# Hybrid decoder layer on one core: a separate transfer path for the modulation of k-tiles 4 to 15

## The chip, the cores and the metric

One core of a Trainium2 chip runs the whole layer as one program. The metric is device time in microseconds, from the start of the program to its end; the median of the runs counts. TensorE multiplies matrices (PE in the profile, with its weight loads as PEld), VectorE (DVE) and ScalarE (ACT) do the elementwise work, GpSimd (POOL) and SyncE (SP) issue transfers here, and POOL builds a few masks as well.

## The reference, cut to what matters

The layer is one block of a decoder: 256 tokens of width 2048, all in float32. A conditioning vector c gives six vectors of modulation, and the first two of them, shift and scale, act on the normalised input of every projection:

```python
mod = (jax.nn.silu(c) @ w_ada[l] + b_ada[l]).reshape(B, N_MOD, 1, D)
sh1, sc1, gt1, sh2, sc2, gt2 = (mod[:, j] for j in range(N_MOD))

h = rmsnorm(x, g_mix[l]) * (1.0 + sc1) + sh1
z = h @ w_in[l]
```

z is cut into the inputs of three token mixers (mLSTM, differential attention, stick-breaking attention) and their gates. Their outputs are projected, gated, summed and projected again, a gated residual is added, and a modulated MLP with a causal convolution follows. w_ada is 2048 x 12288, so the columns that sh1 and sc1 need are 33.5 MB in float32; no column of h can be made before its shift and scale are known, and each needs all 2048 rows of w_ada.

## The kernel before

The width of 2048 is cut into 16 k-tiles of 128. h is kept transposed, one 128 x 256 tile per k-tile, as a high and a low part in a rounded float format; weights are split in the same way, and each product is made of three matmuls (high by high, high by low, low by high). `weights` (L318) loads up to four k-tiles of 512 columns, one megabyte, into one of three buffers (`rawp`), ScalarE writes the high part (L330) and VectorE the low part (L332). A buffer is free again when both have read it.

The modulation takes no TensorE time for its products: `ada_mac` (L208) multiplies the rows of one k-tile of w_ada by the matching entries of silu(c), one number per partition, and adds them up on VectorE over all 16 row tiles; `ada_sums` (L226) then sums over the partitions with one-column matmuls, writes shift and scale, and `make_h` (L438) makes h for the k-tiles concerned.

The columns come in this order. `ada_first(0)` and `ada_first(2)` (L239) give k-tiles 0 and 1, and 2 and 3. `ada_quad` (L260) gives four k-tiles at a time, for k0 = 4, 8 and 12: eight buffers of one megabyte, each of two row tiles of 128 x 1024, filled by two transfers on SyncE's queue (L267), and sixteen multiply-adds. These buffers come from the same `rawp` as the weights, so weights and modulation rotate through the same three in the order of the program, and both go out on SyncE's queue. The accumulators are the two halves of `quads` (slot 4).

Since h arrives piece by piece, the first 13 column blocks of w_in (`first`, L488) are visited several times. `visit` (L531) calls `partial` for a range of blocks up to the k-tile that is there: up to 2, then 4, 8, 12 and 16; the last visit is the loop at L863. The first two blocks keep their sums in PSUM (`kept`), the others add theirs into SBUF (L522). `partial` drives the modulation on if h isn't written far enough (L503).

Two queues of generators, `ada` and `side`, are advanced by `tick` (L200), which is called after each group of four k-tiles and after each block. `rates` say how many steps per tick, 0.72 to 2.1 for `ada` during the visits. Program order is a priority: the planner that comes with the tile framework simulates the program, places each instruction on its engine when the engine is free and its inputs are there in its own time, and fixes an order for each engine. `tc.issue_after` adds a rule to it: an instruction comes after another one on the same engine. The order is kept on the chip: an engine whose next instruction has to wait, waits.

`late_vectors` (L138) loads the small vectors (gains, convolution weights, gate biases, the four lambda vectors) with small transfers on POOL's queue into slot 3 (`rows2`), turns them into columns with five transposes on TensorE, a copy on ScalarE (L164), and computes lambda. It is put on `side` after the third visit (L540). Slot 3 held the first half of x before, and holds the output of stick-breaking attention (`osh`, L550) after it.

Of the kernel before, what the change touches and what calls it, by code (L numbers as in the profile page):

```python
# [10 lines left out]
F32 = mybir.dt.float32  # L11
# [6 lines left out]
P = 128  # L18
S = 256
NT = S // P  # L20
D = 2048
KD = D // P
# [17 lines left out]
def kernel(  # L40
# [6 lines left out]
    nc = tc.nc  # L47
    x2d, out2d = x[0], out[0]
    w_ada, w_in, w_out, w_up, w_down = w_ada[0], w_in[0], w_out[0], w_up[0], w_down[0]
# [4 lines left out]
    rawp = ctx.enter_context(tc.tile_pool(name="rawp", bufs=3))  # L54
# [8 lines left out]
    def slot(i, name):  # L63
        n = NT * MH * (MDH + 1) + 8 if i == 2 else 2048
        return slots.tile([P, n], F32, tag=f"s{i}", name=name)
# [7 lines left out]
    def sidewide(name):  # L73
        return tmp.tile([P, 512], F32, tag="sidewide", name=name, bufs=4)
# [4 lines left out]
    V, A, T = nc.vector, nc.scalar, nc.tensor  # L79
# [58 lines left out]
    def late_vectors():  # L138
        rows = slot(3, "rows2")
        rowsB, rowsC = rows[0:27, 0:P], rows[0:64, P:2 * P]  # L140
        rowsD = rows[0:NF, 2 * P:5 * P].rearrange("k (j p) -> k j p", j=3)
        def ld(*args):
            with tc.issue_after(state["load"].ins):
                nc.gpsimd.dma_start(*args)

        ld(rowsB[0:16], g_ffn[0].rearrange("(k p) -> k p", p=P))
        ld(rowsB[16:24], g_mout[0].rearrange("h (k p) -> (h k) p", p=P))
        ld(rowsB[24:25], g_dsub)
        for r in range(2):
            ld(rowsB[25:26, r * 64:(r + 1) * 64], g_dq)  # L150
            ld(rowsB[26:27, r * 64:(r + 1) * 64], g_dk)
        ld(rowsC, w_mconv[0].rearrange("j (k p) -> (j k) p", p=P))
        ld(rowsD, w_ffconv[0].rearrange("j (k p) -> k j p", p=P))
        ld(bif, b_gate_if.rearrange("o (g h) -> h (o g)", h=MH))
        lamv = rows[0:1, 640:896].rearrange("o (v d) -> o v d", v=4)
        for i, lv in enumerate((lam_q1, lam_k1, lam_q2, lam_k2)):
            ld(lamv[:, i, :], lv)
        yield
        pv = adaps.tile([P, 512], F32, tag="adaps", name="pv")
        T.transpose(pv[:, 0:27], rowsB, ident[:27, :27])  # L160
        T.transpose(pv[:, 27:91], rowsC, ident[:64, :64])
        for j in range(3):
            T.transpose(pv[:, 91 + NF * j:91 + NF * (j + 1)], rowsD[:, j, :], ident[:NF, :NF])
        A.copy(cols, pv[:, 0:223])  # L164
        yield
        V.tensor_scalar(gsub_c, gsub_c, 1.0 - LAM_INIT, None, ALU.mult)
        V.tensor_scalar(gdq_c, gdq_c, 64.0 ** -0.5, None, ALU.mult)

        lp = rows[0:1, 896:1024].rearrange("o (v d) -> o v d", v=2)
        V.tensor_tensor(lp, lamv[:, 0::2, :], lamv[:, 1::2, :], ALU.mult)  # L170
        ls = const.tile([1, 2], F32, name="ls")
        V.tensor_reduce(ls, lp, AX.X, ALU.add)
        A.activation(ls, ls, AF.Exp)
        nl = const.tile([1, 1], F32, name="nl")
        V.scalar_tensor_tensor(nl, ls[:, 1:2], -LAM_INIT, ls[:, 0:1], ALU.add, ALU.subtract)
        yield
        plam = adaps.tile([P, 512], F32, tag="adaps", name="plam")
        T.matmul(plam[:, 0:1], lhsT=ones[0:1, :], rhs=nl, start=True, stop=True)
        V.tensor_copy(nlam, plam[:, 0:1])


    side = deque()
    ada = deque()
    state = {"ada": 0.0, "side": 0.0, "split": None, "load": None, "hold": None, "h": 0, "started": False}
# [13 lines left out]
    rates = {"ada": 0.0, "side": 1.0}  # L198
# [9 lines left out]
    def ada_mac(accs, raw, kt0, nk):  # L208
        for k in range(nk):
            kt = kt0 + k  # L210
            acc = accs[kt % len(accs)]
            if kt < len(accs):
                V.tensor_scalar(acc, raw[:, k, :], ccol[:, kt:kt + 1], None, ALU.mult)
            else:
                state["mac"] = V.scalar_tensor_tensor(acc, raw[:, k, :], ccol[:, kt:kt + 1], acc, ALU.mult, ALU.add)  # L215
# [10 lines left out]
    def ada_sums(accs, k0, nk):  # L226

        pm = adaps.tile([P, 512], F32, tag="adaps", name="pm")
        for i, acc in enumerate(accs):
            for k in range(2 * nk):  # L230
                T.matmul(pm[:, k:k + 1], lhsT=acc[:, k * P:(k + 1) * P], rhs=ones[:, 0:1],  # L231
                         start=k + i == 0, stop=i == len(accs) - 1, skip_group_check=True)
        ks = slice(k0, k0 + nk)
        V.tensor_tensor(b1[:, ks], pm[:, 0:nk], bsh1_c[:, ks], ALU.add)
        V.tensor_tensor(a1[:, ks], pm[:, nk:2 * nk], bsc1_c[:, ks], ALU.add)
        V.tensor_tensor(a1[:, ks], a1[:, ks], gmix_c[:, ks], ALU.mult)
        make_h(k0, k0 + nk)

    def ada_first(k0):  # L239

        accs = [adap.tile([P, 512], F32, tag="acc", name="acc", bufs=2)]
        if k0 == 0:
            accs.append(sidewide("acc2"))
        for q in range(4):
            raw = rawp.tile([P, 4, 512], F32, tag="raw", name="raw")
            step = 2 if k0 == 0 and q == 3 else 4
            for j in range(0, 4, step):
                for i in range(2):
                    r0, c0 = q * 512 + j * P, i * D + k0 * P
                    with tc.issue_after(state["load"].ins) if k0 else nullcontext():  # L250
                        load = nc.sync.dma_start(raw[:, j:j + step, i * 256:(i + 1) * 256],  # L251
                                                 w_ada[r0:r0 + step * P, c0:c0 + 256].rearrange("(k p) f -> p k f", p=P))
            if k0 == 0:
                state["load"] = load
            with tc.issue_after(state["first"].ins) if k0 == 2 and q == 0 else nullcontext():
                ada_mac(accs, raw, 4 * q, 4)
            yield
        ada_sums(accs, k0, 2)

    def ada_quad(k0, acc):  # L260

        for q in range(8):
            raw = rawp.tile([P, 2, 1024], F32, tag="raw", name="raw4")
            for i in range(2):
                r0, c0 = q * 256, i * D + k0 * P
                with tc.issue_after(state["load"].ins):
                    nc.sync.dma_start(raw[:, :, i * 512:(i + 1) * 512],  # L267
                                      w_ada[r0:r0 + 256, c0:c0 + 512].rearrange("(k p) f -> p k f", p=P))
            for k in range(2):
                ada_mac([acc], raw[:, k:k + 1, :], 2 * q + k, 1)  # L270
                yield
        ada_sums([acc], k0, 4)

    def ada_late(comp, g):
# [11 lines left out]
    def ada_columns(comp, bcol, dst, gcol=None):  # L286
        for g in range(4):
            for acc in ada_late(comp, g):
                yield
            pm = partition_sums(acc)  # L290
            ks = slice(4 * g, 4 * g + 4)
            V.tensor_tensor(dst[:, ks], pm[:, 0:4], bcol[:, ks], ALU.add)
            if gcol is not None:
                V.tensor_tensor(dst[:, ks], dst[:, ks], gcol[:, ks], ALU.mult)
# [229 lines left out]

    kept = {}
    quads = slot(4, "quads")
    ada.append(ada_first(2))
    ada.extend(ada_quad(k0, quads[:, (i % 2) * 1024:(i % 2 + 1) * 1024]) for i, k0 in enumerate((4, 8, 12)))
    done = [0] * 13

    def visit(cis, kt1, rate):  # L531
        rates["ada"] = rate
        for ci in cis:
            partial(ci, done[ci], kt1)
            done[ci] = kt1
# [1 line left out]
    visit(range(0, 9), 2, 0.72)  # L537
    visit(range(9, 13), 4, 2.1)
    visit(range(0, 9), 4, 1.1)
    side.append(late_vectors())  # L540
    rates["side"] = 0.4
    visit(range(0, 10), 8, 1.72)
    visit(range(10, 13), 12, 1.36)
    visit(range(0, 7), 12, 1.36)
# [312 lines left out]
    def ada_rest():  # L857
        yield from ada_columns(3, bsh2_c, b2)
        yield from ada_columns(4, bsc2_c, a2, gffn_c)

    ada.append(ada_rest())
    rates["side"] = 2.4
    for ci in range(13):  # L863
        partial(ci, done[ci], 16)
# [20 lines left out]
    for ch in range(2):  # L885
        acc = gemm("T", hact, w_in, 0, C_MO + ch * 512, 512, 0, KD)
# [6 lines left out]
    for ch in range(2):  # L893
        acc = gemm("T", hact, w_in, 0, C_MV + ch * 512, 512, 0, KD)
# [5 lines left out]
    for t, col0, f0 in ((mqT, C_MQ, 0), (mkT, C_MK, 8)):  # L900
        for ch in range(2):
            acc = gemm("H", h1act, w_in, 0, col0 + ch * 512, 512, 0, KD)
# [44 lines left out]
    for ch in range(4):  # L947
        acc = gemm("T", mact, w_out, 0, ch * 512, 512, 0, KD)
# [17 lines left out]
        for k2 in range(2):  # L966
            pb = bank("px2")
            for tt in range(NT):
                for j in range(2):
                    k = 4 * ch + 2 * k2 + j  # L970
                    T.transpose(pb[:, j * S + tt * P:j * S + (tt + 1) * P], x2[tt][:, k * P:(k + 1) * P], ident)
            for j in range(2):
                k = 4 * ch + 2 * k2 + j
# [10 lines left out]
    k = 0  # L984
# [17 lines left out]
    for half, (c0, c1) in enumerate(((0, 6), (6, NCH))):  # L1002
        ath = [slots.tile([P, 8, S], F32R, tag=f"s{i}", name=f"ath{i}") for i in (0, 3, 4)]
        atl = [slots.tile([P, 8, S], F32R, tag=f"s{i}", name=f"atl{i}") for i in (5, 6, 7)]
        for ch in range(c0, c1):
# [21 lines left out]
            i, j0 = (ch - c0) // 2, ((ch - c0) % 2) * 4  # L1027
# [12 lines left out]
        for n in range(4):  # L1040
            acc = gemm("T", act, w_down, c0 * 512, n * 512, 512, 0, 4 * (c1 - c0))
# [37 lines left out]
```

## Time and profile before

| | us |
|---|---|
| runs, median of 3 | 1796.61 (1796.43 to 1796.66) |
| the profiled execution | 1796.63 |
| its span, from first to last instruction | 1794.9 |
| TensorE busy | 1757.0 (98%) |
| VectorE busy | 1325.2 (74%) |
| ScalarE busy | 909.9 (51%) |
| POOL busy | 16.3 (1%) |
| DMA traffic | 423.31 MB, mean 236 GB/s |

Times inside the execution are counted from the start of the span. A busy matmul includes time in which it waits in the pipeline, so a row of busy time is not a row of peak work. "Idle before" is put down to whatever released the engine last. Transfers are shown on the queue of the engine that issues them, with the time from issue to landing.

### The profile page before, as it was taken

How to read it: one execution, taken by the hardware profiler on the slowest of the kernel's cores; microseconds unless marked ns; L12 is line 12 of the kernel's file. 1: busy time of each engine (PE TensorE's matmuls, PEld its weight loads, DVE VectorE, ACT ScalarE, POOL GpSimd, SP SyncE). 2: the span in 40 equal slices, each digit the busy share in tenths (PEclk: the TensorE clock that was granted, in tenths of full speed). 3: DMA queues.
4: the chain of work that ended last, by engine and by line, in shares of the span. 5: the costliest groups of instructions: out<-in, count | busy, mean ns of one | idle time of the engine just before them, and what ended most of it. 6: DMA issues, size and time to landing. Idle time of an engine off the chain costs nothing.

```text
span 1794.9 us, 23561 instructions
## 1 busy us (share of the span) xinstructions
PE 1757.0 (98%) x9101; PEld 1510.3 (84%) x9101; DVE 1325.2 (74%) x1784; ACT 909.9 (51%) x1238; POOL 16.3 (1%) x44
## 2 busy tenths in 40 slices
PE   6999999999999999999999999999999999999998
PEld 5888999888778887888888878888888888888887
DVE  6889766888988678777896577888875556666654
ACT  6533344666565566544444555555553345555432
POOL 2000000000000000000000000000000000000000
PEclk8999999999999999999999999999999999999999
DMA  9989855776777657778896547778755555555563
GB/s 337 356 279 314 299 181 177 241 259 234 247 247 258 199 201 267 237 261 288 308 327 211 186 160 254 248 256 279 269 200 188 199 194 190 190 189 188 187 212 116
DMA packets 219728, 423.31 MB, mean 236 GB/s; under 512 B 9026, under 2 KB 31674, under 8 KB 219104
## 3 DMA queue, kind: packets, MB, share of 16 engines
q1 hardware_dynamic: 217328, 417.44, 68.7%
q0 software_dynamic: 1008, 2.23, 0.4%
q10 hardware_dynamic: 1280, 2.14, 0.3%
q8 instruction: 71, 1.16, 0.3%
q14 instruction: 41, 0.34, 0.0%
HBM read 419.68 MB, written 2.10 MB: 235 GB/s over the span
## 4 chain that ended last, share of the span: by engine, by line
PE 91%; DVE 3%; DMA 3%; ACT 1%; issue 1%; SPq 0%; DVEq 0%; ACTq 0%
PE gp L379 51%; PE acch L365 31%; PE kept L381 2%; PE gp L381 2%; DMA raw<-in_w_in_dram 2%; DVE lo L332 1%; DMA raw<-in_w_ada_dram 1%; DVE quads L215 1%; ACT hi L330 1%; PE psc L650 0%; SPq L251 0%; PE pm L231 0%; DVE acc L215 0%; PE pr L309 0%; PE pmg L848 0%
## 5 line engine op out<-in xcount | busy, mean ns | idle before, releaser
L332 DVE TENSOR_TENSOR lo<-raw,hi 128x1024 fp32r<-128x1024 f32 (+1 forms) x608 | 724.1, 1207 | 344.8 <-ACT hi L330 308.4
L330 ACT CAST hi<-raw 128x1024 fp32r<-128x1024 f32 (+1 forms) x608 | 617.2, 1039 | 608.5 <-PE gp L379 367.0
L379 PE MATMUL gp<-hi,h 128*128 128x512 f32 (+1 forms) x1600 | 408.1, 385 | 6.1 <-ACT hi L330 5.4
L365 PE MATMUL acch<-h,hi 128*128 128x512 f32 x1664 | 404.2, 392 | 1.8 <-DVE h L994 1.8
L365 PEld LDWEIGHTS acch<-h,hi 128*128 128x128 f32 x1664 | 304.7, 189 | 59.9 <-DVE h L994 2.0
L379 PEld LDWEIGHTS gp<-hi,h 128*128 128x128 f32 x1600 | 296.6, 188 | 59.3 <-ACT hi L330 7.2
L379 PE MATMUL gp<-lo,h 128*128 128x512 f32 (+1 forms) x800 | 227.1, 384 | 0.0
L365 PEld LDWEIGHTS acch<-h,lo 128*128 128x128 f32 x1664 | 217.5, 191 | 11.1
L365 PE MATMUL acch<-h,lo 128*128 128x256 f32 x1664 | 220.7, 282 | 0.0
L215 DVE SCALAR_TENSOR_TENSOR acc<-araw,ccol,acc 128x512 f32<-128x512 f32 x240 | 179.1, 747 | 6.5 <-DMA araw<-in_w_ada_dram 4.8
L379 PEld LDWEIGHTS gp<-lo,h 128*128 128x128 f32 x800 | 149.5, 188 | 25.6 <-issue 0.7
L379 PE MATMUL gp<-hi,atl 128*128 128x512 f32 x352 | 136.9, 389 | 0.0
L379 PE MATMUL gp<-hi,ath 128*128 128x512 f32 x352 | 136.8, 389 | 0.0
L379 PE MATMUL gp<-lo,ath 128*128 128x512 f32 x352 | 105.7, 389 | 0.0
L379 PEld LDWEIGHTS gp<-hi,ath 128*128 128x128 f32 x352 | 66.1, 188 | 13.8
L379 PEld LDWEIGHTS gp<-lo,ath 128*128 128x128 f32 x352 | 66.1, 188 | 13.7
L379 PEld LDWEIGHTS gp<-hi,atl 128*128 128x128 f32 x352 | 66.0, 188 | 13.7
L215 DVE SCALAR_TENSOR_TENSOR quads<-raw,ccol,quads 128x1024 f32<-128x1024 f32 x45 | 57.6, 1280 | 2.1 <-DMA raw<-in_w_ada_dram 1.6
L379 PE MATMUL gp<-hi,mgl 128*128 128x512 f32 x128 | 50.3, 393 | 0.0
L379 PE MATMUL gp<-hi,mgh 128*128 128x512 f32 x128 | 50.0, 392 | 0.0
L381 PE MATMUL kept<-h,hi 128*128 128x256 f32 x256 | 42.0, 305 | 5.1 <-ACT hi L330 2.0
L1019 DVE SCALAR_TENSOR_TENSOR y<-gsum,cols,y 128x255 f32<-128x255 f32 (+1 forms) x88 | 41.7, 479 | 4.4 <-ACT y L1017 4.0
(355 smaller groups left out, 1560.8 us busy)
## 6 DMA issues: line engine op xcount, KB each, us to landing
raw<-in_w_in_dram SPq DMA_DIRECT2D x98, 1024.0 KB, 5.1
raw<-in_w_up_dram SPq DMA_DIRECT2D x88, 1024.0 KB, 5.1
araw<-in_w_ada_dram SPq DMA_DIRECT2D x128, 512.0 KB, 5.9
raw<-in_w_down_dram SPq DMA_DIRECT2D x44, 1024.0 KB, 5.1
raw<-in_w_ada_dram SPq DMA_DIRECT2D x62, 512.0 KB, 5.6
raw<-in_w_branch_dram SPq DMA_DIRECT2D x24, 1024.0 KB, 5.2
raw<-in_w_in_dram SPq DMA_DIRECT2D x25, 880.0 KB, 4.7
raw<-in_w_out_dram SPq DMA_DIRECT2D x16, 1024.0 KB, 5.1
```

Of the source, the lines that this page charges most:

```text
L215: state["mac"] = V.scalar_tensor_tensor(acc, raw[:, k, :], ccol[:, kt:kt + 1], acc, ALU.mult, ALU.add)
L330: A.copy(hi[:, :, :n], raw[:, k0:k0 + 2, :n])
L332: state["split"] = V.tensor_tensor(lo[:, :, :n], raw[:, k0:k0 + 2, :n], hi[:, :, :n].bitcast(F32), ALU.subtract)
L365: T.matmul(acc[t][:, 0:m], lhsT=w[k // 2][:, k % 2, sl], rhs=ah(s0 + k)[:, 0:m], start=start, stop=s0 + k == kt1 - 1 and w is (wh if flip ...
L379: T.matmul(o, lhsT=a(s0 + k)[:, sl], rhs=wk[:, :n], **kw)
L381: T.matmul(o, lhsT=wk[:, sl], rhs=a(s0 + k), **kw)
L1019: V.scalar_tensor_tensor(yf[:, sft:S], src[:, 0:S - sft], wc(2 - sft), yf[:, sft:S], ALU.mult, ALU.add)
```

## The change

The twelve k-tiles of `ada_quad` get their own two buffers, the halves of a new tile `quad_raw` in slot 3. Each transfer now carries one row tile, 128 rows of 512 shift columns and 512 scale columns, half a megabyte, and goes out on POOL's queue: 48 such transfers in place of 48 of the same size on SyncE's. The bytes and the 48 multiply-adds are the same. Since a multiply-add empties one buffer, the next transfer but one can start after it.

`ada_first(2)` gets a small memset on VectorE, after the multiply-adds of its third buffer, on one column of each half of `quad_raw`. The first transfer into each half comes after it.

`late_vectors` shares slot 3, so its loads now follow the last read of `quad_raw`. It is put on `side` just ahead of the last visit, where the rate of `side` is 2.4 steps per tick and no longer 0.4. The order rule in its loader is dropped; it named an instruction of another engine.

```diff
         def ld(*args):
-            with tc.issue_after(state["load"].ins):
-                nc.gpsimd.dma_start(*args)
+            nc.gpsimd.dma_start(*args)
...
             with tc.issue_after(state["first"].ins) if k0 == 2 and q == 0 else nullcontext():
                 ada_mac(accs, raw, 4 * q, 4)
+            if k0 == 2 and q == 2:
+                with tc.issue_after(state["mac"].ins):
+                    V.memset(quad_raw[:, :, 0:1], 0.0)
             yield
         ada_sums(accs, k0, 2)
 
     def ada_quad(k0, acc):
 
-        for q in range(8):
-            raw = rawp.tile([P, 2, 1024], F32, tag="raw", name="raw4")
-            for i in range(2):
-                r0, c0 = q * 256, i * D + k0 * P
-                with tc.issue_after(state["load"].ins):
-                    nc.sync.dma_start(raw[:, :, i * 512:(i + 1) * 512],
-                                      w_ada[r0:r0 + 256, c0:c0 + 512].rearrange("(k p) f -> p k f", p=P))
-            for k in range(2):
-                ada_mac([acc], raw[:, k:k + 1, :], 2 * q + k, 1)
-                yield
+        for k in range(KD):
+            raw = quad_raw[:, k % 2:k % 2 + 1, :]
+            nc.gpsimd.dma_start(raw[:, 0, :].rearrange("p (i f) -> p i f", i=2),
+                                w_ada[k * P:(k + 1) * P, 0:2 * D].rearrange("p (i f) -> p i f", i=2)[:, :, k0 * P:k0 * P + 512])
+            ada_mac([acc], raw, k, 1)
+            yield
         ada_sums([acc], k0, 4)
...
     quads = slot(4, "quads")
+    quad_raw = slot(3, "quad_raw").rearrange("p (k f) -> p k f", k=2)
...
     visit(range(0, 9), 4, 1.1)
-    side.append(late_vectors())
-    rates["side"] = 0.4
     visit(range(0, 10), 8, 1.72)
...
     ada.append(ada_rest())
+    side.append(late_vectors())
     rates["side"] = 2.4
     for ci in range(13):
         partial(ci, done[ci], 16)
```

## The prediction

> **What bounds the kernel now.** I read the page's totals first, then the stretches up to the point where the last of the modulation has arrived, then the waits of SyncE's queue, then the chain of waits in the same stretches.
>
> ```profile
> span 1794.9 us, 23561 instructions
> PE 1757.0 (98%) x9101; PEld 1510.3 (84%) x9101; DVE 1325.2 (74%) x1784; ACT 909.9 (51%) x1238; POOL 16.3 (1%) x44
> ```
>
> TensorE is idle for 1794.9 - 1757.0 = 37.9 us of the span, and no more than that can be won. The first step of the modulation, which comes before the first projection matmul, is left as it is, so I looked for the idle time after it, as long as modulation of four k-tiles is still arriving. The stretches (columns: PE, weight loads, DVE, ACT, POOL, granted clock, DMA share, GB/s):
>
> ```profile
> 27.67:50.00 22.33, 22.33 (x136) 20.90 (x136) 20.98 (x30) 11.64 (x18) 1.36 (x3) 0.88 1.07 355
> 50.00:75.00 25.00, 21.58 (x108) 19.35 (x108) 18.30 (x22) 15.09 (x30) 0.00 (x0) 1.00 0.96 336
> 75.00:100.00 25.00, 23.76 (x161) 22.17 (x161) 24.44 (x26) 10.48 (x13) 0.00 (x0) 1.00 1.03 373
> 100.00:125.00 25.00, 21.06 (x125) 18.85 (x124) 23.05 (x35) 9.84 (x15) 0.00 (x0) 0.86 0.74 257
> 125.00:150.00 25.00, 25.00 (x163) 23.02 (x162) 21.29 (x23) 7.77 (x8) 0.00 (x0) 1.00 0.86 286
> 150.00:175.00 25.00, 24.59 (x130) 22.60 (x129) 24.05 (x38) 10.34 (x16) 0.00 (x0) 1.00 0.92 312
> 175.00:205.00 30.00, 27.60 (x144) 25.16 (x142) 23.53 (x27) 10.78 (x12) 0.00 (x0) 1.00 0.94 327
> ```
>
> From the first projection matmul at 27.67 us to 205 us TensorE is busy 165.9 of 177.3 us: 11.4 us are idle. In 100 to 125 us the granted clock is 0.86, which costs up to 0.14 x 25 = 3.5 us more. Together 14.9 us is the ceiling on any gain. Up to 100 us the DMA engines are full (0.96 to 1.07); after that they have room (0.74 to 0.94), and VectorE is nearly full (23.05 and 24.05 of 25 us).
>
> The waits of SyncE's queue, up to 260 us (who, for whom: total, times, longest):
>
> ```profile
> SPq L325 <- DVE lo L332: 91.7, 31, 6.0
> SPq L267 <- DVE lo L332: 33.0, 13, 5.1
> SPq L325 <- DVE quads L215: 30.9, 15, 3.9
> ```
>
> L325 loads weights, L267 the modulation of four k-tiles, and both rotate through the same three buffers. In 15 cases a weight transfer stood until a modulation multiply-add had freed its buffer; in 13 a modulation transfer stood at the head of the queue, with weight transfers behind it. The chain shows what that does:
>
> ```profile
> 107.09 1.14 DVE lo L332
> 108.25 5.11 DMA raw<-in_w_in_dram
> 113.44 1.05 ACT hi L330
> 114.54 11.75 PE kept L381 x82
> ...
> 169.61 1.20 DVE quads L215
> 170.83 5.33 DMA raw<-in_w_in_dram
> 176.26 0.93 ACT hi L330
> 177.24 14.29 PE gp L379 x70
> ```
>
> A buffer is freed, only then does the weight transfer start, and the chain runs through its five microseconds and the split into TensorE. That is the idle time in 100 to 125 us and in 175 to 205 us.
>
> **The change, part by part.** *Weights keep three buffers.* Nothing of the modulation rotates through them after the two early k-tile pairs, and the 48 issues of L267 leave SyncE's queue. At a fixed DMA rate this buys nothing where the DMA share is already about 1, so I count no gain up to 100 us. After it, the idle time of TensorE is 3.94 (100 to 125) + 0.41 (150 to 175) + 2.40 (175 to 205) = 6.75 us, and with the clock's 3.5 us 10.2 us are within reach. VectorE does the same work as before in those stretches and is idle for only 1.95, 0.95 and 6.47 us of them, so I take half: **-5.1 us** (ends 0 and -10.2; -14.9 if the early idle goes too).
>
> *The modulation gets two half-megabyte buffers, on POOL's queue.* Each transfer carries one k-tile, and a buffer's next transfer waits for the multiply-add that empties it. So the pace is set by a loop: issue, landing, wait for VectorE, multiply-add. Durations for it:
>
> ```profile
> L267 SPq DMA_DIRECT2D raw<-in_w_ada_dram x48: 367/413/1100, 37.8 to 197.1; - x48
> DMA to landing us min/median/max: 3.7/4.9/9.2
> L215 DVE SCALAR_TENSOR_TENSOR quads<-raw,ccol,quads x45: 1275/1279/1286, 49.0 to 206.7; 128x1024 f32<-128x1024 f32 x45
> L941 POOL DMA_DIRECT2D x2b<-in_x_dram x1: 585/585/585, 747.0 to 747.0; - x1
> DMA to landing us min/median/max: 5.2/6.5/7.8
> ```
>
> No half-megabyte transfer from POOL's queue is in this trace. The nearest rows are the same bytes from SyncE (median 4.9 us to landing) and one megabyte from POOL (L941's two, 5.2 and 7.8 us, the last row). I take 4.9 plus one POOL issue of 0.6, because the size and the stage are those of the first row: 5.5 us. With the multiply-add (1.28) and half a weight split on VectorE ahead of it (1.22 / 2, the row is below) the loop is 7.4 us, and two buffers give one k-tile per 3.7 us. The bounds: 3.7 + 0.6 + 1.28 = 5.6 us below, 7.8 + 1.28 + 0.6 = 9.7 us above. In the kernel before, the three groups of 16 take 47, 59 and 54 us, 3.3 us a k-tile: **the new loop is slower than what it replaces**, and the question is whether the slack holds it.
>
> ```profile
> 37.67 1.22 DVE L332 TENSOR_TENSOR lo<-raw,hi 128x1024 fp32r<-128x1024 f32 x1
> 39.29 3.12 DVE L215 SCALAR_TENSOR_TENSOR acc<-raw,ccol,acc 128x512 f32<-128x512 f32 x4 [0.40 <-DMA raw<-in_w_ada_dram]
> 95.44 0.75 DVE L213 TENSOR_SCALAR quads<-raw,ccol 128x1024 f32<-128x1024 f32 x1
> 110.33 0.73 PE L381 MATMUL kept<-h,hi 128*128 128x256 f32 x4 [1.72 <-DVE h L404]
> 150.15 1.84 PE L231 MATMUL pm<-ones,quads 128*128 128x1 f32 x16
> 154.08 0.75 DVE L213 TENSOR_SCALAR quads<-raw,ccol 128x1024 f32<-128x1024 f32 x1 [0.37 <-DMA raw<-in_w_ada_dram]
> 157.78 0.42 DVE L404 TENSOR_TENSOR h<-ht,h 128x256 fp32r<-128x256 f32 x1
> 205.40 2.60 DVE L215 SCALAR_TENSOR_TENSOR quads<-raw,ccol,quads 128x1024 f32<-128x1024 f32 x2
> 243.91 11.51 PE kept L381 x96
> ```
>
> The four multiply-adds at 39.29 us are those of the third buffer of the first modulation step (q = 2); they end at 42.4 us, the new memset follows, so the first transfer goes out at about 43 us, where L267's first went out at 37.8. It lands at 48.5. The sixteenth k-tile lands seven loops later, is added by 48.5 + 7 x 7.4 + 2.5 = 103 us (95.4 before), and sums and h take some 4 us (1.84 for the sixteen sums by their row, and an estimated 2 for the short operations behind them; in the second group h is first written 6.2 us after the sums, from 151.99 to 158.20, with other work of VectorE between): 107 us, against TensorE's first use of k-tiles 4 to 7 at 110.3. The thirty-second is added at 103 + 59 = 162 us (154.1 before), h at 166, against the first use of k-tiles 8 to 11 at 177.2 (120 matmuls after the 440-wide blocks begin). The last is added at 221 us (208 before), h at 225, against 243.9, where the last four k-tiles begin. Each date has slack: 3, 11 and 19 us; with the 6.2 in place of the 2, the first is missed by 1 us and the others hold. Cost taken: 0. If VectorE's fixed order puts a multiply-add ahead of its data, a weight split waits behind it, and that is the price of the second rival.
>
> By the Trainium skill's page "DMA: Bandwidth & Descriptors", section "Anatomy of one DMA — SWDGE (gpsimd) path", such a transfer takes 2.0 us plus bytes over 436 GB/s, an estimate of 3.2 us for half a megabyte; the loop would be about 5.1 us, every date would be early, and the result would be the same -5 to -10 us. The row of 4.9 us here is longer, and it decides.
>
> *The gate.* One memset of 128x2 on VectorE: under 0.2 us, nothing. Without it the modulation would start when x has left the slot, about where the first load into that slot now goes out (21.14 us, the first row below).
>
> *The small vectors move behind the last modulation transfer*, because they live in the same slot.
>
> ```profile
> 21.14 0.51 POOL L144 DMA_DIRECT2D rows<-in_g_ffn_dram  x1 [17.31 <-ACT xnT L436]
> 28.55 0.48 POOL L144 DMA_DIRECT2D rows<-in_lam_k_dram  x1
> 101.60 0.24 PE L160 MATMUL pv<-ident,rows 27*128 27x27 f32 x1
> L637 ACT ACTIVATE qdT<-pdt,cols x4: 681/688/697, 422.2 to 423.9; 128x512 f32<-128x512 f32 x4
> L403 ACT CAST osh<-po x4: 585/586/587, 311.3 to 398.7; 128x512 fp32r<-128x512 f32 x4
> ```
>
> Thirteen loads on POOL took 7.9 us from first issue to last; a landing of 5 to 6 us follows. From 221 us they are there at about 235, and the columns are first used at 422, the slot by the next owner at 311. POOL is busy for 16.3 us of the whole span, so the loads delay nothing there. Price taken: 0. But their five transposes sit in TensorE's order, which is fixed before the run; placed ahead of the landing they stop TensorE, for 0 to 14 us. The work itself is moved, not added.
>
> The sum: 1796.63 (the profiled execution's own time, span 1794.9 plus 1.7; the median of the runs is 1796.61) - 5.1 + 0 + 0 = **1791.5 us**.
>
> **Rivals.** *The modulation's loop is the bound (slower).* One place: VectorE waits at L215 for a POOL transfer, and h comes late. It decides when the loop passes about 7.8 us, since the first date has 3 us of slack over 7 loops. At 9.0 us, nearer the POOL rows than SyncE's (landing 7.1): k-tile sixteen at 43 + 7.1 + 63 + 2.5 = 115.6, h at 119.6, 9.3 us late; the next at 191.6 against 177.2 + 9.3, 5.1 more; the last at 263.6 against 258.3, 5.3 more: +19.7, less the 5.1 gained, 1811 us. At 9.7 us it is +36 - 5 = 1827. For it: 7.8 us is a measured POOL landing, at a moment when other transfers were in flight, as they are here. Against it: a slow loop leaves the DMA engines emptier, and 5.2 us for twice the bytes was also measured.
>
> *Nothing to gain.* VectorE is busy for 24.44 of 25 us in 75 to 100, and the DMA engines are full there; the waits of the queue are only the visible end of that. Then the early stretches keep their length, and what is freed later is eaten by modulation that comes later: 1796.6, within 3 us. The Trainium skill says so of the queue alone (same page, "Issuing engines are not separate DMA queues"): transfers from any engine end up on the same 16 DMA engines, and a second issuer saves only issue time. The DMA shares above 0.96 agree up to 100 us; the 0.74 after it does not.
>
> *It doesn't do what it says:* TensorE's order puts the small vectors' transposes too early, and the time won is lost there: -5.1 + up to 14, about 1801.
>
> **How the numbers follow.** A measurement of this kernel can tell about 0.2% (3.6 us) from no change. Forecast (faster, own range 1782 to 1793): 0.46. Loop is the bound (1800 to 1827): 0.28. Nothing to gain: 0.20, of which 0.02 below and 0.01 above the 3.6 us. Late transposes: 0.06, half of it within. That gives faster 0.48, same 0.20, slower 0.32. The range runs from the ceiling of 14.9 us (1781.7, a little lower for the clock before 50 us) to short of the loop's upper bound: 1780 to 1818.
>
> **What would show it.** Right: weight transfers issued earlier than their split needs them, SyncE's waits only on L332, no chain piece of a weight transfer between 100 and 205 us, clock 1.00 in 100 to 125, the last modulation multiply-add near 221 us. Wrong by the first rival: idle time of VectorE at the modulation's multiply-adds put down to its transfer, landings above 6 us on POOL's queue, TensorE idle before 110 and 177 us on h. Wrong by the last: TensorE idle at the small transposes.

## The result, and the profile after

The changed kernel takes 1818.5 us (median of 4 runs, 1817.04 to 1819.72) against 1796.63 us of the kernel before on the same chip (4 runs): a ratio of 1.0119, 95% interval 1.0107 to 1.0132. It is slower by 21.9 us, where 1791.5 us was forecast.

The totals of the page after, with the slices of TensorE:

```profile
span 1817.8 us, 23610 instructions
PE 1761.5 (97%) x9101; PEld 1514.0 (83%) x9101; DVE 1324.7 (73%) x1785; ACT 911.2 (50%) x1238; POOL 51.1 (3%) x92
PE   6949999999999999999999999999999999999998
```

The work is the same, and most of the 22.9 us by which the span grew is idle time of TensorE: 1817.8 - 1761.5 = 56.3 us instead of 37.9. The other 4.5 us are more busy time of as many matmuls, with a lower granted clock in 100 to 150 us (0.71 and 0.75 below). One slice alone, the third, stands at 4. The stretches from 100 us on, as in the prediction (columns: PE, weight loads, DVE, ACT, POOL, granted clock, DMA share, GB/s) put it between 100 and 150 us:

```profile
100.00:125.00 25.00, 7.92 (x34) 6.63 (x34) 15.17 (x21) 2.09 (x2) 5.07 (x7) 0.71 0.69 232
125.00:150.00 25.00, 18.58 (x130) 18.28 (x131) 16.68 (x20) 7.49 (x12) 5.78 (x8) 0.75 0.60 187
150.00:175.00 25.00, 24.05 (x140) 21.06 (x139) 20.44 (x22) 9.44 (x10) 4.48 (x7) 1.00 0.89 295
175.00:205.00 30.00, 28.40 (x147) 26.23 (x148) 25.94 (x39) 12.31 (x18) 5.64 (x8) 1.00 0.85 287
```

TensorE is busy for 7.92 and 18.58 us where it was busy for 21.06 and 25.00. VectorE and the DMA engines are emptier there too, so nothing is short of throughput: something waits. The order of time on TensorE names it (start, duration, line, the idle time before it and its releaser):

```profile
121.07 3.57 PE L230 MATMUL pm<-ones,quads 128*128 128x1 f32 x16 [15.34 <-DVE quads L214]
130.38 1.22 PE L379 MATMUL kept<-h,hi 128*128 128x256 f32 x4 [5.74 <-ACT h L401]
132.65 5.45 PE L379 MATMUL kept<-h,hi 128*128 128x256 f32 x25 [1.04 <-DVE h L402]
```

TensorE stands for 15.34 us until the sixteenth multiply-add of the modulation of k-tiles 4 to 7 is done, and for another 5.74 us until h is made from it. It first uses k-tile 4 at 130.38 us; in the kernel before the first two matmuls with it came at 106.73 us and the next at 110.33 us (both rows are shown further down), so it is 20 to 24 us late. The last four k-tiles begin at 264.90 us in the chain (243.91 before), 21.0 us late, and the span is 22.9 us longer: nearly the whole loss arises at the first of the three dates.

```profile
264.90 5.74 PE kept L379 x48
```

On VectorE, the second and the last of the first group's multiply-adds, and one stretch between them; in the stretch none waits for its transfer:

```profile
55.50 1.28 DVE L214 SCALAR_TENSOR_TENSOR quads<-quad_raw,ccol,quads 128x1024 f32<-128x1024 f32 x1
...
85.17 0.69 DVE L520 SCALAR_TENSOR_TENSOR skT<-gp,skT 128x512 f32<-128x512 f32 x1 [3.62 <-PE gp L379]
85.78 1.22 DVE L330 TENSOR_TENSOR lo<-raw,hi 128x1024 fp32r<-128x1024 f32 x1
...
87.51 1.28 DVE L214 SCALAR_TENSOR_TENSOR quads<-quad_raw,ccol,quads 128x1024 f32<-128x1024 f32 x1
...
112.91 2.60 DVE L214 SCALAR_TENSOR_TENSOR quads<-quad_raw,ccol,quads 128x1024 f32<-128x1024 f32 x2 [2.34 <-DMA quad_raw<-in_w_ada_dram]
119.74 1.28 DVE L214 SCALAR_TENSOR_TENSOR quads<-quad_raw,ccol,quads 128x1024 f32<-128x1024 f32 x1 [4.22 <-DMA quad_raw<-in_w_ada_dram]
```

From 55.50 to 119.74 us are 14 steps, 4.6 us per k-tile or 9.2 us per loop of two buffers. Only the last two rows, the fourteenth and the sixteenth, begin with a wait for a transfer. The one at 87.51 us stands behind sums of z (L520), the first of which waits 3.62 us for TensorE, and behind a weight split: its turn in VectorE's order comes late, and with it the next transfer into its buffer. Its own transfer had gone out at 76.69 us, on POOL, when the multiply-add at 75.11 us had freed the buffer, and landed after 5.1 us, so the data lay ready for 5.7 us; the next transfer into this buffer stood on POOL for 8.01 us until the row at 87.51 was done:

```profile
76.69 0.72 POOL L266 DMA_DIRECT2D quad_raw<-in_w_ada_dram  x1 [4.37 <-DVE quads L214]
...
89.08 0.72 POOL L266 DMA_DIRECT2D quad_raw<-in_w_ada_dram  x1 [8.01 <-DVE quads L214]
```

The transfers' durations, from the rows of their tile:

```profile
L266 POOL DMA_DIRECT2D quad_raw<-in_w_ada_dram x48: 722/722/759, 41.9 to 231.3; - x48
DMA to landing us min/median/max: 3.9/5.6/8.4
```

From issue to landing it is 5.6 us, where 5.5 us were taken for issue and landing together. The Trainium skill's estimate that the prediction gave (page "DMA: Bandwidth & Descriptors", section "Anatomy of one DMA — SWDGE (gpsimd) path", 3.2 us) is too short here; the fastest of the 48 took 3.9 us.

SyncE's queue, up to 260 us, lost the waits that the change was to take away; none is left on a multiply-add of four k-tiles:

```profile
SPq L323 <- DVE lo L330: 165.3, 33, 35.2
```

The longest wait for a split, 35.2 us, is the stall seen from the queue: no weight transfer goes out from 110.6 to 146.2 us, since with TensorE standing no split is made and no buffer comes free.

### The profile page after: what moved, and what is told of

Read it like the earlier page. It is cut to its first block, busy times and chain, and to the rows that moved or that the text cites. A ratio compares the mean times of both kernels' runs of the same rounds, so it can differ in the third digit from the quotient of the medians.

```text
span 1817.8 us, 23610 instructions
## 1 busy us (share of the span) xinstructions
PE 1761.5 (97%) x9101; PEld 1514.0 (83%) x9101; DVE 1324.7 (73%) x1785; ACT 911.2 (50%) x1238; POOL 51.1 (3%) x92
## 4 chain that ended last, share of the span: by engine, by line
PE 90%; DMA 5%; DVE 3%; issue 1%; ACT 1%; SPq 0%; POOL 0%; DVEq 0%; POOLq 0%; ACTq 0%
PE gp L377 50%; PE acch L363 31%; DMA quad_raw<-in_w_ada_dram 3%; PE kept L379 2%; PE gp L379 2%; DVE lo L330 1%; DMA raw<-in_w_ada_dram 1%; DVE quads L214 1%; DMA raw<-in_w_in_dram 1%; PE psc L647 0%; SPq L250 0%; DVE acc L214 0%; ACT hi L328 0%; PE pr L307 0%; PE pm L230 0%
## 5 line engine op out<-in xcount | busy, mean ns | idle before, releaser
L363 PEld LDWEIGHTS acch<-h,lo 128*128 128x128 f32 x1664 | 217.6, 191 | 11.1
L214 DVE SCALAR_TENSOR_TENSOR quads<-quad_raw,ccol,quads 128x1024 f32<-128x1024 f32 x45 | 57.6, 1279 | 34.3 <-DMA quad_raw<-in_w_ada_dram 34.2
L379 PE MATMUL kept<-h,hi 128*128 128x256 f32 x256 | 42.7, 309 | 8.0 <-ACT h L401 5.7
L379 PEld LDWEIGHTS kept<-h,hi 128*128 128x128 f32 x256 | 38.5, 217 | 8.6 <-ACT h L401 5.8
```

Source lines behind the costliest of these rows:

```text
L363: T.matmul(acc[t][:, 0:m], lhsT=w[k // 2][:, k % 2, sl], rhs=ah(s0 + k)[:, 0:m], start=start, stop=s0 + k == kt1 - 1 and w is (wh if flip ...
L379: T.matmul(o, lhsT=wk[:, sl], rhs=a(s0 + k), **kw)
```

## The experiments

The questions were which part of the change costs the time (the two buffers, the queue, the later small vectors), and whether the two-buffer loop is long because data is late or because VectorE's order is. Line numbers shift a little between the kernels: L379 and L380, or L401 and L402, are the same line of the program. A ratio is to the kernel before, run beside it on the same chip, with its 95% interval; the runs come from several chips, so they are compared by their ratios.

**Small vectors alone.** The kernel before, with `late_vectors` put behind the last modulation:

```diff
-    side.append(late_vectors())
-    rates["side"] = 0.4
...
     ada.append(ada_rest())
+    side.append(late_vectors())
```

> The kernel before, with only the small vectors moved to just ahead of the last visit; the modulation keeps the weights' three buffers and SyncE's queue. Theory A (two buffers of half a megabyte are too few, the first group of sixteen comes late): the small vectors cost nothing, 1796.6 within 2 us. Theory C (the moved transposes or loads stop TensorE): 1805 or more, with TensorE idle at the small transposes.

Measured: 1796.8 us, 1.0006 (0.9997 to 1.0016). The small vectors cost nothing, as the prediction said. This run moves their transposes, but its loads still go out before 30 us, since nothing else holds slot 3. In the changed kernel their thirteen loads go out from 240.97 us on, and TensorE isn't idle before their transposes at 256.7 us.

**The queue alone.** The kernel before with its shared buffers; only the engine that issues the modulation changes, and with it the order rule goes, which names an instruction on SyncE's queue:

```diff
-                with tc.issue_after(state["load"].ins):
-                    nc.sync.dma_start(raw[:, :, i * 512:(i + 1) * 512],
+                if True:
+                    nc.gpsimd.dma_start(raw[:, :, i * 512:(i + 1) * 512],
```

> The kernel before, with only the modulation's transfers (same size, same three shared buffers) issued on POOL's queue. Theory A: the queue matters little, 1796 to 1800, first use of k-tile 4 by TensorE still near 110 us. Theory B (POOL's queue lands too slowly): 1808 or more, with VectorE waiting on these transfers and the first use of k-tile 4 past 118 us.

Measured: 1803.48 us, 1.0046 (1.0030 to 1.0061), between the two expectations. The execution whose rows follow was the longest of the five (1809.22 us; the others took 1801.62 to 1805.04), so the waits shown are on the long side. POOL's issues in order of time, and the stretch that they fall in:

```profile
51.08 1.44 POOL L267 DMA_DIRECT2D raw<-in_w_ada_dram  x2 [12.77 <-DMA raw<-in_w_in_dram]
65.31 1.44 POOL L267 DMA_DIRECT2D raw<-in_w_ada_dram  x2 [12.79 <-DVE lo L332]
...
50.00:75.00 25.00, 22.41 (x88) 20.18 (x88) 14.32 (x19) 11.74 (x24) 4.32 (x6) 0.77 0.75 237
```

With the buffers still shared, POOL's queue stands 12.8 us ahead of each of these two pairs of transfers, for a weight's own transfer and split in the buffer that comes next. The DMA share in 50 to 75 us is 0.75 (0.96 before), and k-tile 4 is first used at 117.54 us. The queue of its own costs time already without the two buffers.

**The two buffers alone.** The changed kernel with its modulation on SyncE's queue:

```diff
-            nc.gpsimd.dma_start(raw[:, 0, :].rearrange("p (i f) -> p i f", i=2),
+            nc.sync.dma_start(raw[:, 0, :].rearrange("p (i f) -> p i f", i=2),
```

> The changed kernel with the modulation's two buffers of its own, but the transfers issued on SyncE's queue. Theory A: still slow, 1812 to 1822, TensorE idle for more than 12 us ahead of k-tile 4. Theory B: the loss is gone, 1793 to 1800.

Measured: 1809.43 us, 1.0076 (1.0061 to 1.0091), below the range of theory A, with the stall that it named. The stall is shorter, and k-tile 4 comes at 122.2 us:

```profile
114.88 3.58 PE L230 MATMUL pm<-ones,quads 128*128 128x1 f32 x16 [9.15 <-DVE quads L214]
122.16 2.93 PE L379 MATMUL kept<-h,hi 128*128 128x256 f32 x12 [3.70 <-ACT h L401]
```

**Four buffers, taken from the weights.** The changed kernel with a second pair of buffers in a slot more, paid for by weights that rotate through two buffers in place of three:

```diff
-    rawp = ctx.enter_context(tc.tile_pool(name="rawp", bufs=3))
+    rawp = ctx.enter_context(tc.tile_pool(name="rawp", bufs=2))
...
-            raw = quad_raw[:, k % 2:k % 2 + 1, :]
+            raw = (quad_raw, quad_raw2)[k // 2 % 2][:, k % 2:k % 2 + 1, :]
```

> The changed kernel with four half-megabyte buffers for the modulation in place of two, paid with one of the weights' three buffers. Theory A: the loop has twice the transfers in flight, the sixteenth multiply-add is back near 95 to 100 us and the loss of 20 us at k-tile 4 is gone; with weights down to two buffers 1794 to 1803. Theory B: landing on POOL's queue still sets the pace, 1808 or more.

Measured: 1812.83 us, 1.0100 (1.0083 to 1.0117). TensorE no longer waits for the sums, but for weights (7.0 us in five waits for their high parts). Two things were changed at once, so this run says little of the modulation's buffers.

**Four buffers, weights with their three.** The second pair is laid into the slot of `sqT`, which nothing else uses before the last visit; first on POOL's queue, as in the changed kernel, then on SyncE's:

```diff
+    quad_raw2 = sqT.rearrange("p (k f) -> p k f", k=2)
...
-            raw = quad_raw[:, k % 2:k % 2 + 1, :]
+            raw = (quad_raw, quad_raw2)[k // 2 % 2][:, k % 2:k % 2 + 1, :]
```

> The changed kernel with four half-megabyte buffers for the modulation (the two halves of the slot of sqT, which is not written before the last visit, are the other two), weights keeping three, transfers on POOL's queue. Theory A (two buffers are too few): the sixteenth multiply-add moves from 119.7 to about 100 us, the first use of k-tile 4 from 130 to 110 to 114 us, and 17 to 21 us of the loss go: 1796 to 1801. Theory D (buffers and queue each cost by themselves, 14 and 7 us, as the single steps showed): only the buffers' part goes, 1801 to 1806.

> The same four buffers beside the weights' three, transfers on SyncE's queue: one megabyte more in flight than before and no POOL. Theory A and D: no loss left, 1790 to 1798. If the modulation's transfers on SyncE's queue hold weight transfers up while they wait for their buffer: 1798 to 1804.

Measured: 1802.18 us, 1.0036 (1.0023 to 1.0049) on POOL's queue, as theory D had it (k-tile 4 comes at 119.8 us there), and 1792.24 us, 0.9978 (0.9969 to 0.9988) on SyncE's. The latter's order of time on TensorE:

```profile
99.94 1.95 PE L230 MATMUL pm<-ones,quads 128*128 128x1 f32 x16
109.80 0.74 PE L380 MATMUL kept<-h,hi 128*128 128x256 f32 x4
113.53 4.67 PE L380 MATMUL kept<-h,hi 128*128 128x256 f32 x25 [3.00 <-DVE h L403]
```

With four buffers on SyncE's queue nothing waits for the sums, and k-tile 4 is in use from 109.80 us on, 3 us later than in the kernel before; what is left is 3.00 us on the last of h. Together with the runs above this makes a table of ratios, in which buffers and queue add up to within the intervals (some 3 us each):

| modulation's buffers | SyncE's queue | POOL's queue | the queue's price |
|---|---|---|---|
| shared with the weights | 1 (before) | 1.0046 | 8.3 us |
| two of its own | 1.0076 | 1.0119 (the change) | 7.7 us |
| four of its own | 0.9978 | 1.0036 | 10.4 us |

(A price is the difference of the ratios times 1796.6.) Two buffers in place of four cost 17.6 us on SyncE's queue and 14.9 us on POOL's.

**The first group on the old path.** The changed kernel, with k-tiles 4 to 7 through the shared buffers and SyncE's queue, and only k-tiles 8 to 15 through two buffers on POOL's; the gate's memset follows the sixteenth multiply-add:

```diff
+        if k0 == 4:
+            for q in range(8):
+                raw = rawp.tile([P, 2, 1024], F32, tag="raw", name="raw4")
...
+            return
```

> The changed kernel with the first group of four k-tiles (4 to 7) on the old path (three shared buffers, SyncE's queue) and only the other two groups through the two buffers on POOL's queue. If the loss is the first date alone (k-tile 4 used 20 us late): 1793 to 1799. If the slow loop costs at the later dates too: 1803 or more, with TensorE idle ahead of k-tile 8 or 12.

Measured: 1798.49 us, 1.0016 (1.0006 to 1.0025), k-tile 4 in use from 107.7 us on. The two later dates hold with two buffers on POOL's queue; 18.5 us (1.0119 - 1.0016 of 1796.6) of the loss go with the first.

**Multiply-adds in program order.** In the changed kernel 30 weight splits stand ahead of the sixteenth multiply-add in VectorE's fixed order (23 in the kernel before, both counted from the start of the program). Here each split of the first group is ordered behind the multiply-add issued before it in the program, and 22 are left:

```diff
+            if k:
+                state["quad"] = state["mac"]
...
-            with tc.issue_after(hold.ins) if hold else nullcontext():
+            pin = hold or (state.get("quad") if state["h"] == 4 else None)
+            with tc.issue_after(pin.ins) if pin else nullcontext():
```

> The changed kernel, with VectorE's order forced for the first group: a weight split comes after the modulation multiply-adds that stand ahead of it in the program (the sixteenth then stands behind 22 weight splits and not 30). Theory O (the data is there, the fixed order keeps the multiply-adds waiting): the first group is done near 105 us, 1803 to 1810. Theory L (landing and two buffers set the pace): the wait only moves to the weight splits, VectorE's waits for these transfers go from 34 us to over 50, 1816 to 1826.

Measured: 1805.99 us, 1.0057 (1.0042 to 1.0072), 11.1 us (0.0062) less than the change. First group on VectorE, and the stretches:

```profile
55.43 1.28 DVE L214 SCALAR_TENSOR_TENSOR quads<-quad_raw,ccol,quads 128x1024 f32<-128x1024 f32 x1
...
105.22 1.28 DVE L214 SCALAR_TENSOR_TENSOR quads<-quad_raw,ccol,quads 128x1024 f32<-128x1024 f32 x1
...
75.00:100.00 25.00, 15.50 (x88) 13.78 (x87) 15.61 (x14) 4.94 (x7) 5.06 (x7) 0.86 0.79 267
100.00:125.00 25.00, 23.35 (x132) 20.88 (x131) 25.00 (x38) 11.05 (x16) 4.36 (x7) 0.94 0.70 240
```

The 14 steps take 49.8 us, a loop of 7.1 us: with its turn on VectorE secured, the loop has the length that was predicted (7.4). But now VectorE waits for modulation (16.5 us in 11 waits from 40 to 125 us) with weight splits behind it, and TensorE is idle for 9.5 us in 75 to 100 us. With two buffers on POOL's queue the choice is between a late modulation and late weights.

**The same order, four buffers, both queues.** The order rule of the last run on top of four buffers, on POOL's queue and then on SyncE's. Up to the sixteenth multiply-add, VectorE's order is then the same in both but for the first four multiply-adds, which stand earlier with SyncE's queue.

> Two buffers more for the modulation, as in the run with four buffers and weights on three, POOL's queue, and in addition each weight split in the first group of modulation is ordered behind the multiply-add that the program issued before it, so that the sixteenth multiply-add stands behind 22 splits in VectorE's fixed order instead of 27. If the 9.9 us between POOL's queue and SyncE's, with the same four buffers, come from where the multiply-adds stand in VectorE's fixed order, TensorE first uses k-tile 4 near 110 to 113 us (119.8 without the order) and the time is 1792 to 1797. If they come from the queue itself (later issue, longer landing), k-tile 4 stays at 117 us or later, VectorE waits longer at its multiply-adds for their transfers (3.2 us without the order), and the time stays at 1799 to 1804.

> The run with four buffers, POOL's queue and the forced order (1798.9 us, 1.0009 of the kernel before), with SyncE's queue in place of POOL's; VectorE's order is the same but for the first two multiply-adds. If the rest of the price of POOL's queue is in the queue (it takes as large a share of the DMA engines as the weights, whose transfers then land after 12 to 14 us), the time is 1791 to 1794 (0.997 to 0.999), with weights landing in 9 to 10 us. If the whole price was in VectorE's order, both queues give the same time under the same order: 1797 to 1801.

Measured: 1798.87 us, 1.0009 (1.0000 to 1.0018) on POOL's queue and 1792.54 us, 0.9977 (0.9967 to 0.9986) on SyncE's. The order alone won 0.0027 on POOL's queue, 4.9 us, and nothing on SyncE's; 5.7 us (0.0032) are left to the queue, with those four places. The transfers of 50 to 110 us (size, median to landing) and each queue's share of the DMA engines, on POOL's queue:

```profile
q1 hardware_dynamic: 5418, 9.97, 47.1%
q0 software_dynamic: 2841, 10.32, 47.1%
...
quad_raw<-in_w_ada_dram POOLq DMA_DIRECT2D x10, 512.0 KB, 7.0
raw<-in_w_in_dram SPq DMA_DIRECT2D x5, 512.0 KB, 12.1
```

and on SyncE's:

```profile
quad_raw<-in_w_ada_dram SPq DMA_DIRECT2D x10, 512.0 KB, 9.3
raw<-in_w_in_dram SPq DMA_DIRECT2D x5, 512.0 KB, 9.6
```

The modulation lands sooner on its own queue and the weights later: 12.1 in place of 9.6 us for half a megabyte and 13.6 in place of 11.2 us for a whole one, with both queues at 47.1% of the engines. (The other four weight transfers, of 440 and 880 KB, land sooner instead.) What a late weight does to TensorE is seen with POOL's queue:

```profile
94.77 1.04 ACT L331 CAST hi<-raw 128x1024 fp32r<-128x1024 f32 x1 [11.45 <-DMA raw<-in_w_in_dram]
...
95.87 1.22 PE L383 MATMUL gp<-h,hi 128*128 128x256 f32 x4 [6.43 <-ACT hi L331]
```

That weight transfer went out at 79.2 us and took 15.5 us. Its like with SyncE's queue went out at 78.5 us, when VectorE was as far with the modulation (the eleventh multiply-add at 79.1 and 80.0 us), and took 9.6 us. In 75 to 100 us TensorE is busy for 18.53 us with POOL's queue and for 21.80 us with SyncE's. The Trainium skill (page "DMA: Bandwidth & Descriptors", section "Queues, rings and completion order") says that each DMA engine takes turns between the queues that have work for it, packet by packet. The equal shares of time don't show that rule: the bytes were nearly equal too (9.97 and 10.32 MB), and the packets were not (5418 and 2841).

**Sums first.** The changed kernel with the next group's first multiply-add ordered behind the last step that makes h:

```diff
-            ada_mac([acc], raw, k, 1)
+            with tc.issue_after(state["made"].ins) if k0 > 4 and k == 0 else nullcontext():
+                ada_mac([acc], raw, k, 1)
```

> The changed kernel, with the first multiply-add of each next group ordered behind the last step that makes h of the group before, so that no multiply-add whose data is still under way stands ahead of the short operations that make h. The path from the sixteenth multiply-add to h is 10 us in the changed kernel, where the prediction took 4. If the two multiply-adds of the next group that stand in it cause this (one of them waited 3.5 us for its transfer), k-tile 4 is first used near 125 us instead of 130.4 and the time is 1812 to 1815. If other work of VectorE fills the same place, or the next group's delay gives it back, the time stays within 2 us of 1818.

Measured: 1820.83 us, 1.0132 (1.0118 to 1.0145), which is not clear of the change's 1.0119 (1.0107 to 1.0132). The order does what it should at the first date, and nothing is left of it at the last:

```profile
125.65 6.31 PE L380 MATMUL kept<-h,hi 128*128 128x256 f32 x28 [2.43 <-ACT h L402]
...
256.54 2.21 PE L230 MATMUL pm<-ones,quads 128*128 128x1 f32 x16 [1.46 <-DVE quads L214]
263.37 5.54 PE L380 MATMUL kept<-h,hi 128*128 128x256 f32 x26 [4.62 <-ACT h L402]
```

k-tile 4 comes at 125.65 us, 4.7 us earlier, but each group now starts later, and the third is done at 256.5 us instead of 241.0 in the changed kernel, when TensorE already waits for it: 1.46 and 4.62 us.

**No gate.** The changed kernel without its memset of 128x2, so that its loop may begin when x has left the slot:

```diff
-            if k0 == 2 and q == 2:
-                with tc.issue_after(state["mac"].ins):
-                    V.memset(quad_raw[:, :, 0:1], 0.0)
```

> The changed kernel without the 128x2 memset, so that modulation of four k-tiles may start its transfers as soon as x has left the slot (about 21 us instead of 42). If the late start of the loop is what matters, the two first transfers come 20 us earlier, beside the first step's loads, and k-tile 4 is first used some 5 to 9 us earlier, at 121 to 125 us, with a time of 1810 to 1814. If the loop's pace and the fixed order set the date, the early transfers only wait in their buffers: the time stays within 3 us of 1818, or is longer if they delay the first step (its last multiply-adds, first projection matmul at 27.7 us).

Measured: 1809.81 us, 1.0071 (1.0057 to 1.0085), 8.6 us (0.0048) less than the change.

```profile
L263 POOL DMA_DIRECT2D quad_raw<-in_w_ada_dram x48: 722/722/757, 20.8 to 229.9; - x48
...
114.59 3.57 PE L230 MATMUL pm<-ones,quads 128*128 128x1 f32 x16 [3.17 <-DVE quads L214]
122.69 6.01 PE L376 MATMUL kept<-h,hi 128*128 128x256 f32 x29 [4.53 <-ACT h L398]
```

The first transfer goes out at 20.8 us, two k-tiles are added before the gate would open, and k-tile 4 comes 7.7 us earlier. The memset costs 0.06 us itself; what it holds back costs more than that.

**The version that beats both.** Four buffers, SyncE's queue, and the next group ordered behind the making of h:

> Four buffers for the modulation, SyncE's queue (1792.2 before) and the next group's first multiply-add ordered behind the making of h of the group before. If the path from the sums to h still holds TensorE at the first date (3.0 us on h in the run without this order), the time is 1788 to 1791. If TensorE's remaining idle time lies elsewhere, it stays at 1791 to 1794.

Measured: 1787.84 us (5 runs), 0.9949 (0.9936 to 0.9963): 9 us faster than the kernel before, 30 us (0.0170) less than the change.

```profile
100.00:125.00 25.00, 23.61 (x173) 22.44 (x173) 24.32 (x36) 11.13 (x17) 0.00 (x0) 1.00 0.71 250
125.00:150.00 25.00, 25.00 (x142) 22.65 (x141) 24.27 (x29) 9.25 (x10) 0.00 (x0) 1.00 0.98 342
150.00:175.00 25.00, 25.00 (x133) 23.59 (x133) 20.02 (x31) 11.87 (x18) 0.00 (x0) 1.00 0.82 273
175.00:205.00 30.00, 30.00 (x195) 28.95 (x195) 27.66 (x30) 12.36 (x13) 0.00 (x0) 1.00 0.99 351
```

From 100 to 205 us TensorE is idle for 1.4 us, and the clock is 1.00. The order that won nothing on two buffers wins on four (0.0029, 5.2 us, against the run without it). That the groups that follow have room with four buffers is the likely reason; no run tests it alone.

## Why the prediction was wrong

The forecast of -5.1 us failed, and the first rival, the loop as the bound, is what happened. The forecast's figures for the first date:

| step | predicted | after |
|---|---|---|
| first transfer goes out | 43 us | 41.9 us |
| issue and landing | 5.5 us | 5.6 us |
| first multiply-add | 48.5 us | 52.6 us |
| loop of two k-tiles | 7.4 us | 9.2 us |
| sixteenth added | 103 us | 121.0 us |
| from there to h in use | 4 us | 9.4 us |
| h of k-tile 4 | 107 us | 130.4 us |

*The loop.* The step that failed is the forecast's term for VectorE's turn, "half a weight split on VectorE ahead of it", 0.6 us. Landing (5.6) and multiply-add (1.28) were right, so of 9.2 us about 2.3 are left for the turn; measured from the landing of each transfer to the start of its multiply-add, the mean over the second to the sixteenth is 2.1 us. Late turns made the multiply-adds wait their place while their data lay ready, and only the last rows of the group waited for a transfer; with the order forced the loop was 7.1 us. The late start is the same: the first transfer landed at 49.0 us and its multiply-add came at 52.6. Start and loop together are 18 us of the 23.4 by which h was late.

*The slack.* The path from the last multiply-add to h was put at "some 4 us", and with the 6.2 us of another group as the worse case. The first group's own rows in the trace before would have said more:

```profile
95.92 1.84 PE L231 MATMUL pm<-ones,quads 128*128 128x1 f32 x16
106.73 0.46 PE L381 MATMUL kept<-h,hi 128*128 128x256 f32 x2
110.33 0.73 PE L381 MATMUL kept<-h,hi 128*128 128x256 f32 x4 [1.72 <-DVE h L404]
```

The prediction took the row at 110.33 for the first use of k-tile 4. The first use is the row at 106.73, two matmuls with the high part of h, and the row at 110.33 begins after a wait of 1.72 us for the low part. So TensorE was already waiting at the first date, and there was no slack of 3 us: h at 107 us would have been late by itself. From the end of the sums at 97.8 us it is 9.0 us to the first use and 12.6 us to the second in the kernel before. A path that takes 9 to 13 us in VectorE's order isn't shortened by its operations being short.

In the changed kernel part of this path is two multiply-adds of the next group, which wait for their own transfers ahead of the additions that make h:

```profile
125.44 1.28 DVE L214 SCALAR_TENSOR_TENSOR quads<-quad_raw,ccol,quads 128x1024 f32<-128x1024 f32 x1 [3.53 <-DMA quad_raw<-in_w_ada_dram]
126.64 0.15 DVE L233 TENSOR_TENSOR b<-pm,colsA 128x4 f32<-128x4 f32 x1
...
127.06 1.28 DVE L214 SCALAR_TENSOR_TENSOR quads<-quad_raw,ccol,quads 128x1024 f32<-128x1024 f32 x1 [0.20 <-DMA quad_raw<-in_w_ada_dram]
128.26 0.15 DVE L235 TENSOR_TENSOR a<-a,colsA 128x4 f32<-128x4 f32 x1
```

*The gain.* The waits of weights on modulation went, as predicted, but what they were worth could not come while TensorE waited for h. That there were 10.2 us within reach was about right: the version with four buffers, SyncE's queue and one more order rule won 9.2 us (0.0051 x 1796.6), with TensorE nearly gapless in the stretches that were named. It is another change than the one forecast, so it doesn't bear out the -5.1 us.

*The later dates.* The slack of 11 and 19 us at the second and third date held but for little: since all of TensorE's work moved by some 20 us, it waits 0.75 us for the sums of the second group and not at all for those of the third. The first rival's 5.1 and 5.3 us for these dates did not come.

*The queue.* The prediction costed the own queue by its landing alone and found it nearly neutral. It costs 8 to 10 us, shown in three pairs of runs. With four buffers about half of it is VectorE's order, which the planner lays out otherwise when POOL issues (27 splits ahead of the sixteenth multiply-add, 23 with SyncE), and the rest stays under one order of splits, with the weights' later landing as what the rows show of it. With the two buffers of the change itself it looks otherwise. There 30 splits stand ahead of the sixteenth multiply-add on either queue, and the weights that go out in 50 to 110 us land hardly later on POOL's (medians of 5.8 us for half a megabyte and 8.1 us for a whole one, 6.7 and 7.7 us on SyncE's). The third multiply-add comes at 60.6 us with POOL's queue and at 60.3 us with SyncE's, the sixteenth at 119.7 and 113.5 us: 4.5 and 4.1 us per k-tile. So neither more splits nor later weights explain the price there, and its cause stays open.

*The first rival* had the mechanism and its sign, at a time of 1811 us. It took the length of the loop from a landing of 7.1 us. The landing was 5.6; the turn on VectorE made up the difference, and the path to h came on top. So its loop of 9.0 us met the measured 9.2 us by luck.

*The second rival*, nothing to gain, counted on a second issuer that costs nothing; the three pairs speak against that, and the version that won 9.2 us against there being nothing to gain. The third, late transposes, did not occur.

*The gate* was given no price beyond its memset, with a start at 43 us. As long as the first date binds, that start is worth 8.6 us. *The small vectors* cost nothing, as predicted, and their transposes stop nothing.

## What to carry to other kernels

The pace of a double-buffered stream includes the turn of the consumer in its engine's fixed order: read it from the spacing of the consumer's rows in the trace, not from durations, and read the slack of a date from the wait in the row that uses the data. A buffer more pays where the consumer's turn is irregular; taking streams apart pays only if each still has enough buffers to cover that. An own queue under full DMA load is also a choice of who lands first; with four buffers it favoured the modulation, and the weights' delay was what TensorE felt. And a change of the issuing engine can change the order that is planned for other engines: compare that order before blaming the queue.

## What was not expected of the hardware

With the 15.3 us of idleness the clock granted to TensorE fell to 0.50, where it stayed from 112 to 136 us; from 138 us on it was 1.00 again. So it was still halved for 15 us after the sums began at 121 us: the sixteen sums took 3.57 us instead of 1.84, and a stall costs more than its own length.

Half-megabyte transfers landed on POOL's queue no later than on SyncE's (medians of 5.6 us in the change and 5.7 us with its modulation on SyncE's queue), although an issue occupies POOL for 0.72 us and SyncE's queue for 0.37.
